# Two-input SBUF operations of a convolutional feed-forward: GpSimd's share given to VectorE, one convolution step to ScalarE

## The chip, the cores and the metric

The kernel runs on one core of a Trainium2 chip. The metric is the device time of one execution, in microseconds (us). A core has TensorE (PE, with its weight loads as PEld), VectorE (DVE), ScalarE (ACT), GpSimd (POOL) and SyncE (SP), each of which takes the instructions of its own queue in order.

## The reference, cut to what matters

Two attention layers and one mixing layer come first; the change lies in the last block, a feed-forward with a causal convolution of three taps over time:

```python
D_FF, FFN_CONV = 2816, 3
def conv_ffn(h, w_up, conv_w, conv_b, w_down):      # h: 1024 x 1024
    up, gv = jnp.split(h @ w_up, 2, axis=-1)        # w_up: 1024 x 5632
    up = causal_dwconv(up, conv_w, conv_b)          # y[t] = b + sum_i w[i] x[t-2+i], per channel
    return (jax.nn.gelu(up) * gv) @ w_down          # w_down: 2816 x 1024
# x = x + conv_ffn(rmsnorm(x, mlp_norm), ...); return rmsnorm(x, final_norm)
```

## The kernel before, in words

All arithmetic keeps float32 accuracy: an operand is split into a rounded part (`...h`, cast by ScalarE) and the rest (`...l` = operand minus rounded part, one two-input subtraction), and `mm3` (L125) issues three matmuls for a product (L127 to L129).

Both products of the feed-forward use seven block products in place of eight (a Strassen-Winograd scheme), so there are sums of blocks besides the splits. `up_sums` (L2076) makes the four sums of the activations once, T1 to T4, in four steps `k`; each step writes its sums into one tile `tz` of which there is a single buffer (tag `fxs`), and splits them into `ft1h/l` to `ft4h/l`. `ffn` (L2109) then goes through 11 rounds `j` of 256 channels. Round 0 is computed with plain products (`plain`, L2179). In each later round, for the half that is convolved (`i = 0`) and the gate half (`i = 1`): `load` fetches a 1 MB block `wraw` of the weights (two buffers), `sums` (L2137) makes the block sums in place and four splits `w1` (1024 columns), `ws2`, `ws1` (512 each), `w3` (1024) and `w4` (512) through `split_up` (L2032), and `prods` (L2158) issues 84 matmuls and takes the results out of PSUM into `fup` or `fg` with copies on ScalarE and sums on VectorE (L2167, L2173, L2175). The convolution (L2210 to L2212) and the gelu (L2213) follow for two tiles of 128 x 1024, then the sums of the down-weights `draw` (L2220 to L2223; the tile shares the one `fxs` buffer), the product with the gate (L2228), the sums of the result (L2231 to L2234) and the stores to DRAM tiles `fx` and `fy`.

The down product (L2259 on) loads one 128 x 512 piece of each operand per step `k` (`drx`, `dry`), splits both (`operands`, L2262), multiplies into eight PSUM banks (`fda`, `fdb`) and ends with the final norm (`final_norm`, L2041).

The order of the instructions on each engine is not that of the text: a scheduler orders them at build time by an estimate of when each can start. Tiles are reused through semaphores, per tile.

Before the change GpSimd has: the splits of `w1`, `ws1` and `w3` and those of `plain` and of the two weight blocks split ahead in the mixing layer (L2038); T3 and the splits of T3 and T4; the four `draw` sums; the split of the second operand of the down product (`dyl`, L2272); and two small memsets per round and a product of the final norm, which stay.

Of the kernel before, what the change touches and what calls it, by code (L numbers as in the profile page):

```python
# [12 lines left out]
F32 = mybir.dt.float32  # L13
F32R = mybir.dt.float32r
I32 = mybir.dt.int32
AF = mybir.ActivationFunctionType
ALU = mybir.AluOpType
# [35 lines left out]
class Kern:  # L53
# [1975 lines left out]
            yh, yl = H[k // 4, n]  # L2029
            self.mm3(o, w[0][:, k], w[1][:, k], yh[:, k % 4], yl[:, k % 4], k == 0, k == 7)  # L2030

    def split_up(self, W, raw, bufs, eng=None):  # L2032
        nc = self.nc
        n = raw.shape[1]
        wh = W.tile([128, 8, 128], F32R, name="fwh", tag="fwh", bufs=bufs)[:, 0:n]
        wl = W.tile([128, 8, 128], F32R, name="fwl", tag="fwl", bufs=bufs)[:, 0:n]
        nc.scalar.copy(wh, raw)  # L2037
        (eng or nc.gpsimd).tensor_tensor(wl, raw, wh.bitcast(F32), ALU.subtract)  # L2038
        return wh, wl

    def final_norm(self, W, t, x, g, out):  # L2041
# [33 lines left out]

    def up_sums(self, R, H):  # L2076

        nc, V, G = self.nc, self.nc.vector, self.nc.gpsimd
        new = lambda nm: R.tile([128, 4, 512], F32R, name=nm)
        T = {i: (new(f"ft{i}h"), new(f"ft{i}l")) for i in (2, 1, 3, 4)}  # L2080

        def split(i, k, t, eng):
            h, l = T[i]
            nc.scalar.copy(h[:, k], t)
            eng.tensor_tensor(l[:, k], t, h[:, k].bitcast(F32), ALU.subtract)

        def steps(P):
            for k in range(4):
                y11h, y11l, y21h, y21l, y22h, y22l, y12h, y12l = (
                    z[:, k].bitcast(F32) for b in ((0, 0), (1, 0), (1, 1), (0, 1)) for z in H[b])  # L2090
                z = P.tile([128, 4, 512], F32, name="tz", tag="fxs", bufs=1)
                t1, t2, t3, t4 = (z[:, i] for i in range(4))
                V.tensor_tensor(t1, y12h, y11h, ALU.subtract)
                V.tensor_tensor(t1, t1, y12l, ALU.add)
                V.tensor_tensor(t1, t1, y11l, ALU.subtract)
                V.tensor_tensor(t2, y22h, t1, ALU.subtract)
                V.tensor_tensor(t2, t2, y22l, ALU.add)
                split(2, k, t2, V)
                split(1, k, t1, V)
                G.tensor_tensor(t3, y22h, y12h, ALU.subtract)  # L2100
                G.tensor_tensor(t3, t3, y22l, ALU.add)
                G.tensor_tensor(t3, t3, y12l, ALU.subtract)
                split(3, k, t3, G)
                V.tensor_tensor(t4, y21h, t2, ALU.subtract)
                V.tensor_tensor(t4, t4, y21l, ALU.add)
                split(4, k, t4, G)
        return T, steps

    def ffn(self, h, side, x_src, out):  # L2109
        nc, a, sm = self.nc, self.a, self.sm  # L2110
        V, G = nc.vector, nc.gpsimd
# [5 lines left out]
        xd = [self.dr.tile([128, 7, 512], F32, name=f"fx{j}") for j in range(NJ)]  # L2117
        yd = [self.dr.tile([128, 4, 512], F32, name=f"fy{j}") for j in range(NJ)]
        with self.pool("fw", not side) as FW:
# [3 lines left out]
            cw = F1.tile([128, 22, 3], F32, name="fcw")  # L2123
            nc.sync.dma_start(cw, a["mlp_conv_w_2"])
            cb = F1.tile([128, 22], F32, name="fcb")
# [11 lines left out]
            def sums(j, i, raw):  # L2137

                b = lambda g, f: raw[:, 4 * g:4 * g + 4, f * 128:f * 128 + 128]
                x11, x12, x21, x22 = b(0, 0), b(1, 0), b(0, 1), b(1, 1)  # L2140
                s2, s1 = b(2, 0), b(2, 1)
                fa = raw[:, 0:8, 0:128]
                w1 = self.split_up(F0, fa, 2)
                V.tensor_tensor(s1, x21, x22, ALU.add)
                V.tensor_tensor(s2, s1, x11, ALU.subtract)
                w2 = self.split_up(FW, s2, 2, V), self.split_up(FW, s1, 2)
                V.tensor_tensor(x21, x11, x21, ALU.subtract)
                w3 = self.split_up(F0, raw[:, 0:8, 128:256], 2)
                V.tensor_tensor(s2, x12, s2, ALU.subtract)
                w4 = self.split_up(FW, s2, 2, V)  # L2150
                return w1, w2, w3, w4

            def mm4(o, w, k0, y, first):
# [40 lines left out]
            for j in range(NJ):  # L2194
                if j:
                    raws = [load(j, 0), load(j, 1)]
                ups = [F1.tile([128, S + 2], F32, name="fup", tag="fup", bufs=2) for _ in range(2)]
                for u in ups:
                    G.memset(u[:, 0:2], 0.0)
                gs = [F1.tile([128, S], F32, name="fg", tag="fg", bufs=2) for _ in range(2)]  # L2200
                if j == 0:
                    t_steps(F1)
                    plain([ups[0][:, 2:], ups[1][:, 2:], gs[0], gs[1]])
                else:
                    prods(j, 0, sums(j, 0, raws[0]), ups[0][:, 2:], ups[1][:, 2:])
                cvs = []
                for i, up in enumerate(ups):
                    f = 2 * j + i
                    cv = F1.tile([128, S], F32, name="fcv", tag="fcv", bufs=2)
                    V.tensor_scalar(cv, up[:, 2:], cw[:, f, 2:3], cb[:, f:f + 1], ALU.mult, ALU.add)  # L2210
                    V.scalar_tensor_tensor(cv, up[:, 1:S + 1], cw[:, f, 1:2], cv, ALU.mult, ALU.add)
                    V.scalar_tensor_tensor(cv, up[:, 0:S], cw[:, f, 0:1], cv, ALU.mult, ALU.add)  # L2212
                    nc.scalar.activation(cv, cv, AF.Gelu_apprx_tanh)  # L2213
                    cvs.append(cv)

                z = F1.tile([128, 4, 512], F32, name="draw", tag="fxs", bufs=1)
                nc.sync.dma_start(z.rearrange("p (f n) c -> p f (n c)", f=2),
                                  wdn[j * 256:j * 256 + 256, :].rearrange("(f p) n -> p f n", p=128))
                y11, y12, y21, y22 = (z[:, q] for q in range(4))
                G.tensor_tensor(y11, y12, y11, ALU.subtract)  # L2220
                G.tensor_tensor(y12, y22, y12, ALU.subtract)  # L2221
                G.tensor_tensor(y22, y22, y11, ALU.subtract)
                G.tensor_tensor(y21, y21, y22, ALU.subtract)  # L2223
                nc.scalar.dma_start(yd[j], z)
                if j:
                    prods(j, 1, sums(j, 1, raws[1]), gs[0], gs[1])
                for cv, g in zip(cvs, gs):
                    V.tensor_tensor(cv, cv, g, ALU.mult)  # L2228
                z = F1.tile([128, 4, 512], F32, name="fxs", tag="fxs", bufs=1)
                x11, x21, x12, x22 = (cv[:, n * 512:n * 512 + 512] for cv in cvs for n in range(2))  # L2230
                V.tensor_tensor(z[:, 0], x21, x22, ALU.add)  # L2231
                V.tensor_tensor(x21, x11, x21, ALU.subtract)
                V.tensor_tensor(z[:, 1], z[:, 0], x11, ALU.subtract)
                V.tensor_tensor(z[:, 2], x12, z[:, 1], ALU.subtract)  # L2234
                for q, t in enumerate((cvs[0], cvs[1])):
                    nc.scalar.dma_start(xd[j][:, 2 * q:2 * q + 2].rearrange("p n c -> p (n c)"), t)
                nc.scalar.dma_start(xd[j][:, 4:7], z[:, 0:3])
# [5 lines left out]
            prod = [(0, wy(0, 0), "A", True, 0, 0), (2, wy(1, 0), "B", True, 0, 0), (5, ty(3), "A", False, 0, 1),  # L2243
                    (4, ty(0), "B", True, 1, 1), (1, ty(1), "A", False, 1, 1), (6, wy(1, 1), "B", False, 0, 1),
                    (3, ty(2), "A", False, 1, 0)]

            pre = []
            for k in range(2):
                raw = FW.tile([128, 12, 256], F32, name="wraw", tag="wraw", bufs=2)
# [9 lines left out]
            with self.pool("dn", side) as DN, self.psum(A=(1, 4), B=(1, 4)):  # L2259
                xa, acc = [], {}  # L2260

                def operands(q, k):  # L2262
                    if q == 0 and k < 2:
                        return pre[k]
                    res = []
                    for nm, src, eng in (("x", xd[k][:, prod[q][0]], V), ("y", prod[q][1](k), G)):
                        raw = DN.tile([128, 512], F32, name="dr" + nm, tag="dr" + nm, bufs=6)
                        nc.sync.dma_start(raw, src)
                        hi = DN.tile([128, 512], F32R, name=f"d{nm}h", tag=f"d{nm}h", bufs=13)
                        lo = DN.tile([128, 512], F32R, name=f"d{nm}l", tag=f"d{nm}l", bufs=13)  # L2270
                        nc.scalar.copy(hi, raw)  # L2271
                        eng.tensor_tensor(lo, raw, hi.bitcast(F32), ALU.subtract)  # L2272
                        res.append((hi, lo))
                    return res

# [11 lines left out]
                for q in range(6):  # L2287
# [13 lines left out]
                    for t in range(4):  # L2301
                        read(q, t)
                ops = [operands(6, k) for k in range(NJ)]

                def last(t):
# [133 lines left out]
```

## Time and profile before

| | |
|---|---|
| time, 3 runs | 2934.91 us median (2933.06 to 2941.24) |
| the profiled execution | 2937.08 us, of which the span from first to last instruction is 2935.3 us |
| TensorE busy | 2734.4 us, 93% of the span |
| VectorE busy | 1924.4 us, 66% |
| ScalarE busy | 1298.2 us, 44% |
| GpSimd busy | 1130.4 us, 39% |
| mean granted TensorE clock | 0.964 of full speed |

Times in the rows are in us from the start of the span; "mean ns" is for one instruction. The feed-forward begins at about 2220 us: the activations' sums and round 0 up to about 2300, rounds 1 to 10 up to about 2705, the down product from there to the end.

### The profile page before, as it was taken

The page shows a single profiled execution, that of the slowest core. Times are in us where ns is not written, and L with a number is a line of the kernel's source. Part 1 is how long each engine was busy: PE and PEld are TensorE (multiplying, and loading weights), DVE is VectorE, ACT ScalarE, POOL GpSimd, SP SyncE. Part 2 cuts the span into 40 slices and gives each one's busy share as a digit, 9 for nine tenths or more (in the row PEclk, how much of TensorE's full clock was granted, in tenths as well). Part 3 has the DMA queues.
Part 4 walks back from the last instruction along what each step waited for, and adds up shares of the span by engine and source line. Part 5 has one row for each costly group of instructions (what it writes and reads, how often), then busy time and mean ns, then how long its engine had stood idle before and what let it go on. Part 6 is the DMA issues. An engine that isn't in the chain of part 4 may idle for free. (4 is left out here: it accounts for less than half of the span.)

```text
span 2935.3 us, 42585 instructions
## 1 busy us (share of the span) xinstructions
PE 2734.4 (93%) x14978; PEld 2191.2 (75%) x14978; DVE 1924.4 (66%) x4235; ACT 1298.2 (44%) x2534; POOL 1130.4 (39%) x851
## 2 busy tenths in 40 slices
PE   7999999899998999989999998999998899998998
PEld 6987666676778998766767775798676677776787
DVE  4784627785567676367866568643688688886733
ACT  5562227675623652156767323224333233323544
POOL 2232215672222324136742204341205555455743
PEclk9999999999999999999999999899999899999999
DMA  7456762326573363534056732245531334443973
GB/s 225 110 138 209 210 173 78 108 71 166 172 264 100 100 168 100 159 111 112 33 150 182 254 120 74 83 110 180 185 109 51 133 144 151 152 156 143 332 208 108
DMA packets 316602, 427.61 MB, mean 146 GB/s; under 512 B 36658, under 2 KB 224162, under 8 KB 314980
## 3 DMA queue, kind: packets, MB, share of 16 engines
q1 hardware_dynamic: 294464, 366.91, 41.9%
q10 hardware_dynamic: 21924, 57.98, 5.1%
q8 instruction: 118, 1.93, 0.3%
q14 instruction: 96, 0.79, 0.1%
HBM read 291.55 MB, written 132.64 MB: 145 GB/s over the span
## 5 line engine op out<-in xcount | busy, mean ns | idle before, releaser
L794 ACT ACTIVATE P<-P,nb 128x1024 f32<-128x1024 f32 (+1 forms) x320 | 316.6, 991 | 119.4 <-DVE nb L787 93.1
L127 PE MATMUL pj<-wh,hh 128*128 128x384 f32 (+3 forms) x768 | 264.4, 346 | 1.8 <-ACT cr L624 1.0
L128 PE MATMUL pj<-wl,hh 128*128 128x384 f32 (+3 forms) x768 | 263.7, 344 | 0.0
L129 PE MATMUL pj<-wh,hl 128*128 128x384 f32 (+3 forms) x768 | 260.8, 344 | 0.0
L806 PE MATMUL ptp<-ident,P 128*128 128x128 f32 x1568 | 218.4, 277 | 9.0 <-ACT PT L808 5.7
L806 PEld LDWEIGHTS ptp<-ident,P 128*128 128x128 f32 x1568 | 180.1, 142 | 50.8 <-issue 19.1
L2038 POOL TENSOR_TENSOR fwl<-wraw,fwh 128x1024 fp32r<-128x1024 f32 (+1 forms) x64 | 157.7, 2465 | 116.9 <-ACT fwh L2037 116.9
L954 POOL TENSOR_TENSOR P<-P,cf 128x1024 f32<-128x1024 f32 x64 | 121.0, 1893 | 211.4 <-DVE cf L952 147.3
L162 POOL TENSOR_TENSOR wl<-raw,wh 128x384 fp32r<-128x384 f32 (+3 forms) x64 | 77.7, 1218 | 300.2 <-ACT wh L161 257.3
L808 ACT COPY PT<-ptp 128x512 f32<-128x512 f32 (+1 forms) x255 | 138.1, 554 | 68.7 <-PE ptp L806 51.2
L787 DVE CUSTOM_DVE_ANT_0 P<-sd,zero 128x1024 f32<-128x1024 f32 x128 | 153.8, 1216 | 20.3 <-PE sd L945 20.0
L127 PE MATMUL po<-wh,yh 128*128 128x512 f32 x384 | 153.2, 406 | 8.2 <-ACT yh L1548 5.0
L129 PE MATMUL po<-wh,yl 128*128 128x512 f32 x384 | 152.2, 403 | 5.3 <-DVE yl L1549 5.3
L128 PE MATMUL po<-wl,yh 128*128 128x512 f32 x384 | 154.4, 402 | 1.3 <-DVE wl L140 1.2
L955 POOL TENSOR_TENSOR P<-P 128x1024 f32<-128x1024 f32 x64 | 153.5, 2402 | 3.6
L128 PEld LDWEIGHTS pj<-wl,hh 128*128 128x128 f32 x768 | 146.1, 190 | 10.7 <-issue 5.2
L127 PEld LDWEIGHTS pj<-wh,hh 128*128 128x128 f32 x768 | 146.1, 190 | 9.0 <-ACT cr L624 1.3
L129 PEld LDWEIGHTS pj<-wh,hl 128*128 128x128 f32 x768 | 145.1, 190 | 8.1 <-issue 3.5
L2037 ACT CAST fwh<-wraw 128x512 fp32r<-128x512 f32 (+1 forms) x104 | 83.2, 801 | 150.8 <-PE fu L128 90.2
L787 DVE CUSTOM_DVE_ANT_0 P<-sm,zero 128x1024 f32<-128x1024 f32 x96 | 116.9, 1218 | 44.5 <-PE sm L129 38.1
L2272 POOL TENSOR_TENSOR dyl<-dry,dyh 128x512 fp32r<-128x512 f32 x75 | 109.7, 1477 | 84.6 <-ACT dyh L2271 84.4
L2272 DVE TENSOR_TENSOR dxl<-drx,dxh 128x512 fp32r<-128x512 f32 x75 | 79.9, 1091 | 92.6 <-ACT dxh L2271 88.6
(724 smaller groups left out, 7777.2 us busy)
## 6 DMA issues: line engine op xcount, KB each, us to landing
adaw<-in_ada_w_dram SPq DMA_DIRECT2D x48, 512.0 KB
wraw<-in_w_up_dram SPq DMA_DIRECT2D x20, 1024.0 KB
raw<-in_w_in_dram SPq DMA_DIRECT2D x76, 256.0 KB
drx<-fx SPq DMA_DIRECT2D x75, 256.0 KB
mn<-naT SPq DMA_DIRECT2D x72, 256.0 KB
nab<-in_na_rpb_dram SPq DMA_DIRECT2D x24, 576.0 KB
naT<-sgn SPq DMA_DIRECT2D x64, 192.0 KB
md<-dfT SPq DMA_DIRECT2D x96, 128.0 KB
```

What stands on the lines that cost most here:

```text
L127: mm(o, lh, rh, start=first, stop=False, **kw)
L128: mm(o, lh, rl, start=False, stop=False, **kw)
L129: mm(o, ll, rh, start=False, stop=last, **kw)
L787: nc.vector.tensor_tensor_reduce(out=P[:, :n], in0=src, in1=self.zero.to_broadcast([128, n]), op0=ALU.add, op1=ALU.min, scale=1.0, scalar= ...
L794: nc.scalar.activation(P[:, :n], P[:, :n], AF.Exp, bias=nb, scale=-1.0 if bias is None else 1.0, accum_out=sums)
L806: nc.tensor.transpose(T[:, j * 128:(j + 1) * 128], P[:, (c + j) * 128:(c + j + 1) * 128], self.ident)
L808: e(PT[:, c:c + m, q, :], T[:, 0:m * 128].rearrange("p (k t) -> p k t", k=m))
L954: nc.gpsimd.tensor_tensor(Ps[1], Ps[1], cf[:, 1:2].to_broadcast([128, S]), ALU.mult)
L955: nc.gpsimd.tensor_tensor(Ps[0], Ps[0], Ps[1], ALU.add)
L2037: nc.scalar.copy(wh, raw)
L2038: (eng or nc.gpsimd).tensor_tensor(wl, raw, wh.bitcast(F32), ALU.subtract)
L2272: eng.tensor_tensor(lo, raw, hi.bitcast(F32), ALU.subtract)
```

## The change

All two-input operations on SBUF tiles that GpSimd did in the feed-forward go to VectorE: the remaining splits of `split_up`, T3 and the splits of T3 and T4, the `draw` sums, and `dyl`. The convolution's first step (scale by a per-channel weight and add the bias) goes from VectorE to an activation with function Identity on ScalarE. Counts, tiles, buffers and transfers stay.

```diff
-    def split_up(self, W, raw, bufs, eng=None):
+    def split_up(self, W, raw, bufs):
...
         nc.scalar.copy(wh, raw)
-        (eng or nc.gpsimd).tensor_tensor(wl, raw, wh.bitcast(F32), ALU.subtract)
+        nc.vector.tensor_tensor(wl, raw, wh.bitcast(F32), ALU.subtract)
...
-        def split(i, k, t, eng):
+        def split(i, k, t):
             h, l = T[i]
             nc.scalar.copy(h[:, k], t)
-            eng.tensor_tensor(l[:, k], t, h[:, k].bitcast(F32), ALU.subtract)
+            V.tensor_tensor(l[:, k], t, h[:, k].bitcast(F32), ALU.subtract)
...
-                G.tensor_tensor(t3, y22h, y12h, ALU.subtract)
-                G.tensor_tensor(t3, t3, y22l, ALU.add)
-                G.tensor_tensor(t3, t3, y12l, ALU.subtract)
-                split(3, k, t3, G)
+                V.tensor_tensor(t3, y22h, y12h, ALU.subtract)
+                V.tensor_tensor(t3, t3, y22l, ALU.add)
+                V.tensor_tensor(t3, t3, y12l, ALU.subtract)
+                split(3, k, t3)
...
-                split(4, k, t4, G)
+                split(4, k, t4)
...
-                w2 = self.split_up(FW, s2, 2, V), self.split_up(FW, s1, 2)
+                w2 = self.split_up(FW, s2, 2), self.split_up(FW, s1, 2)
...
-                    V.tensor_scalar(cv, up[:, 2:], cw[:, f, 2:3], cb[:, f:f + 1], ALU.mult, ALU.add)
+                    nc.scalar.activation(cv, up[:, 2:], AF.Identity, bias=cb[:, f:f + 1], scale=cw[:, f, 2:3])
...
-                G.tensor_tensor(y11, y12, y11, ALU.subtract)
-                G.tensor_tensor(y12, y22, y12, ALU.subtract)
-                G.tensor_tensor(y22, y22, y11, ALU.subtract)
-                G.tensor_tensor(y21, y21, y22, ALU.subtract)
+                V.tensor_tensor(y11, y12, y11, ALU.subtract)
+                V.tensor_tensor(y12, y22, y12, ALU.subtract)
+                V.tensor_tensor(y22, y22, y11, ALU.subtract)
+                V.tensor_tensor(y21, y21, y22, ALU.subtract)
...
-                    for nm, src, eng in (("x", xd[k][:, prod[q][0]], V), ("y", prod[q][1](k), G)):
+                    for nm, src in (("x", xd[k][:, prod[q][0]]), ("y", prod[q][1](k))):
...
-                        eng.tensor_tensor(lo, raw, hi.bitcast(F32), ALU.subtract)
+                        V.tensor_tensor(lo, raw, hi.bitcast(F32), ALU.subtract)
```

## Rows read from the trace of the kernel before

**Rows 1.** The page's first part: busy time, share of span, instructions.
```profile
PE 2734.4 (93%) x14978; PEld 2191.2 (75%) x14978; DVE 1924.4 (66%) x4235; ACT 1298.2 (44%) x2534; POOL 1130.4 (39%) x851
```

**Rows 2.** Windows of the feed-forward: from:to, length, busy (instructions), clock, DMA.
```profile
core 0: us, PE busy (x) PEld busy (x) DVE busy (x) ACT busy (x) POOL busy (x), PEclk, DMA share, GB/s
...
2220.00:2260.00 40.00, 39.22 (x168) 31.30 (x168) 39.72 (x32) 15.30 (x21) 26.20 (x15) 1.00 0.23 69
2260.00:2300.00 40.00, 19.48 (x59) 14.19 (x60) 32.08 (x28) 12.13 (x20) 24.85 (x15) 0.66 0.18 64
...
2300.00:2700.00 400.00, 374.74 (x1588) 301.49 (x1587) 318.41 (x287) 131.10 (x189) 214.44 (x120) 0.98 0.41 148
2700.00:2745.00 45.00, 36.81 (x131) 28.85 (x131) 17.07 (x17) 15.30 (x25) 16.32 (x12) 0.84 0.82 306
2745.00:2936.00 191.00, 182.95 (x805) 151.05 (x803) 95.35 (x142) 91.27 (x175) 104.37 (x72) 0.98 0.60 191
```

**Rows 3.** Timeline of PE: start, duration, line, [idle before <-releaser].
```profile
2272.93 0.80 PE L127 MATMUL fc<-ft1h,fwh 128*128 128x512 f32 x1 [13.71 <-ACT fwh L2037]
...
2286.69 0.80 PE L127 MATMUL fu<-ft2h,fwh 128*128 128x512 f32 x1 [3.65 <-DVE fup L2167]
...
2337.84 0.80 PE L127 MATMUL fu<-ft2h,fwh 128*128 128x512 f32 x1 [5.05 <-DVE fup L2167]
...
2490.49 0.50 PE L129 MATMUL fu<-y00h,fwl 128*128 128x512 f32 x1 [1.70 <-POOL fwl L2038]
...
2531.17 0.50 PE L129 MATMUL fu<-y00h,fwl 128*128 128x512 f32 x1 [1.75 <-POOL fwl L2038]
```

**Rows 4.** Timeline of DVE, from round 2 and a steady round.
```profile
2330.51 3.34 DVE L2212 SCALAR_TENSOR_TENSOR fcv<-fup,fcw,fcv 128x1024 f32<-128x1024 f32 x1
2333.78 3.41 DVE L2228 TENSOR_TENSOR fcv<-fcv,fg 128x1024 f32<-128x1024 f32 x1
...
2464.53 3.07 DVE L2228 TENSOR_TENSOR fcv<-fcv,fg 128x1024 f32<-128x1024 f32 x1 [0.34 <-ACT fg L2177]
...
2468.24 0.68 DVE L2038 TENSOR_TENSOR fwl<-wraw,fwh 128x512 fp32r<-128x512 f32 x1
...
2471.25 1.78 DVE L2234 TENSOR_TENSOR fxs<-fcv,fxs 128x512 f32<-128x512 f32 x1
...
2477.39 1.28 DVE L2212 SCALAR_TENSOR_TENSOR fcv<-fup,fcw,fcv 128x1024 f32<-128x1024 f32 x1
...
2498.35 1.22 DVE L2228 TENSOR_TENSOR fcv<-fcv,fg 128x1024 f32<-128x1024 f32 x1
```

**Rows 5.** Timeline of POOL in the same steady round.
```profile
2464.09 2.43 POOL L2038 TENSOR_TENSOR fwl<-wraw,fwh 128x1024 fp32r<-128x1024 f32 x1 [2.82 <-ACT fwh L2037]
2470.68 1.80 POOL L2038 TENSOR_TENSOR fwl<-wraw,fwh 128x512 fp32r<-128x512 f32 x1 [4.16 <-ACT fwh L2037]
...
2481.30 1.29 POOL L2220 TENSOR_TENSOR draw<-draw 128x512 f32<-128x512 f32 x1 [2.46 <-issue]
...
2487.09 3.34 POOL L2038 TENSOR_TENSOR fwl<-wraw,fwh 128x1024 fp32r<-128x1024 f32 x1
```

**Rows 6.** Waits between 2300 and 2700: who for whom, total us, times, longest.
```profile
POOL fwl L2038 <- ACT fwh L2037: 113.6, 29, 9.0
...
DVE fwl L2038 <- PE fc L129: 27.3, 8, 3.5
...
PE fu L129 <- POOL fwl L2038: 13.1, 7, 2.6
```

**Rows 7.** Groups of DVE between 2300 and 2700: busy us, mean ns of one.
```profile
L2210 DVE TENSOR_SCALAR fcv<-fup,fcw,fcb 128x1024 f32<-128x1024 f32 x20 | 27.0, 1352 | 7.4 <-ACT fup L2177 7.2
```

**Rows 8.** Groups of ACT over the whole span.
```profile
L2213 ACT ACTIVATE fcv<-fcv 128x1024 f32<-128x1024 f32 x22 | 23.3, 1061 | 123.4 <-DVE fcv L2212 123.3
...
L207 ACT ACTIVATE xs<-xs,xrs 128x1024 f32<-128x1024 f32 x4 | 4.4, 1139 | 0.0
```

**Rows 9.** Groups from 2700 to the end: the down product's split on POOL.
```profile
L2272 POOL TENSOR_TENSOR dyl<-dry,dyh 128x512 fp32r<-128x512 f32 x75 | 109.7, 1477 | 84.6 <-ACT dyh L2271 84.4
```

More of the change, by code (lines that the diff above doesn't have):

```diff
@@ L2076, in up_sums @@
     def up_sums(self, R, H):
-        nc, V, G = self.nc, self.nc.vector, self.nc.gpsimd
+        nc, V = self.nc, self.nc.vector
         new = lambda nm: R.tile([128, 4, 512], F32R, name=nm)
         T = {i: (new(f"ft{i}h"), new(f"ft{i}l")) for i in (2, 1, 3, 4)}
-        def split(i, k, t, eng):
+        def split(i, k, t):
             h, l = T[i]
             nc.scalar.copy(h[:, k], t)
-            eng.tensor_tensor(l[:, k], t, h[:, k].bitcast(F32), ALU.subtract)
+            V.tensor_tensor(l[:, k], t, h[:, k].bitcast(F32), ALU.subtract)
         def steps(P):
@@ L2097, in steps @@
                 V.tensor_tensor(t2, t2, y22l, ALU.add)
-                split(2, k, t2, V)
-                split(1, k, t1, V)
-                G.tensor_tensor(t3, y22h, y12h, ALU.subtract)
-                G.tensor_tensor(t3, t3, y22l, ALU.add)
-                G.tensor_tensor(t3, t3, y12l, ALU.subtract)
-                split(3, k, t3, G)
+                split(2, k, t2)
+                split(1, k, t1)
+                V.tensor_tensor(t3, y22h, y12h, ALU.subtract)
+                V.tensor_tensor(t3, t3, y22l, ALU.add)
+                V.tensor_tensor(t3, t3, y12l, ALU.subtract)
+                split(3, k, t3)
                 V.tensor_tensor(t4, y21h, t2, ALU.subtract)
                 V.tensor_tensor(t4, t4, y21l, ALU.add)
-                split(4, k, t4, G)
+                split(4, k, t4)
         return T, steps
@@ L2149, in sums @@
                 V.tensor_tensor(s2, x12, s2, ALU.subtract)
-                w4 = self.split_up(FW, s2, 2, V)
+                w4 = self.split_up(FW, s2, 2)
                 return w1, w2, w3, w4
```

## The prediction, as it was written before the result

> **What bounds the kernel now.** I read the page's first part, then windows of the stretch that the change touches, then the timelines of TensorE, VectorE and GpSimd there, and last the table of waits. The page says that TensorE is busy 93% of the span [rows 1], so only TensorE's idle time and its slow time can be won, and the other engines count only through them. The windows say where that is [rows 2]: from 2220 to 2300, 21.3 of 80 us are idle (80 minus 39.22 and 19.48); from 2300 to 2700, 25.3 of 400 are; from 2700 to 2745, 8.2 of 45; after it 8.1 of 191, which lie in the final norm's tail, where nothing changes. The reader should see in the same rows the granted clock: 0.66 from 2260 to 2300 and full speed before. That window begins to starve TensorE (one wait of 13.71 us [rows 3]) and the clock is low behind it, so idle time costs twice. At full clock 168 matmuls took 39.22 us, 0.233 each; 59 took 19.48 in the slow window instead of 13.8, a loss of 5.7. For 2300 to 2700 I price the slow time by the clock, 0.98: 2% of 374.74 is 7, of which I count 5, since the rounding allows 3.7 to 9. What can be won is thus 21.3 + 5.7 = 27 in the first stage and 25.3 + 5 = 30 in the rounds, 57 in all.
>
> Who holds TensorE up? Steady rounds begin 40.7 us apart (2490.49 to 2531.17), and the one stall in each is 1.7 us for the rest part of a weight split that GpSimd makes [rows 3]; seven of these make 13.1 us [rows 6]. In the early rounds it waits for VectorE: 5.05 us at 2337.84 for a sum (L2167) [rows 3] that stood on VectorE behind an L2212 of 3.34 and an L2228 of 3.41 us [rows 4]. In the first stage it waits for the sums T and for a cast that stands on ScalarE behind casts of T [rows 3].
>
> The last thing to see is that VectorE is slow when GpSimd works. The same L2228 takes 3.07 us at 2464.53, where GpSimd subtracts from 2464.09 to 2466.52, and 1.22 at 2498.35 where GpSimd is idle; a 512-column sum takes 1.78 at 2471.25, with GpSimd at work from 2470.68 to 2472.48, and 0.68 at 2468.24 without [rows 4, 5]. GpSimd suffers too: its 1024-column split takes 2.43 or 3.34 us [rows 5].
>
> **The change part by part.** *The rounds.* From the code, VectorE has in a round 22 operations of 512 columns, two L2228, four convolution steps L2211 and L2212, and two L2210. Alone these cost 22 x 0.68 + 2 x 1.22 + 4 x 1.28 = 22.5 us [rows 4], and L2210 2 x 1.35 as it stands now [rows 7]: 25.2. It is in fact busy 318.41 / 400 x 40.7 = 32.4 us a round [rows 2], so some 7 us of a round are stretch. The change adds six operations of 512 columns (two `ws1`, four `draw`) and four of 1024 (`w1`, `w3`): 6 x 0.68 + 4 x 1.22 = 9.0 us. It takes L2210 away. With GpSimd left with only memsets, VectorE needs 22.5 + 9.0 = 31.5 of 40.7 us: about what it is busy now, for more work. So no new bound by the sum.
>
> What it gives TensorE: a 1024-column split comes 1.22 us after its cast in place of 2.43 to 3.34, and is not behind a `draw` sum on GpSimd; the gain in latency, 1.2 to 2.1, is as large as the stall of 1.7. I take 11 of the 13.1 us. The other 12.2 of idle time in the rounds (25.3 - 13.1) are waits like that at 2337.84; there the two stretched operations ahead of the sum shrink by 2.06 + 2.19 = 4.2 us, against a wait of 5.05. I take 9 of 12.2, and 3 of the 5 us of slow clock with them: 23.
>
> What is new: VectorE takes its queue in order. A `draw` sum now stands in it until its transfer has landed; GpSimd stood 2.46 us for that at 2481.30 [rows 5]. What is queued behind are splits and the sum L2167 that TensorE wants next. Per round the cost is nothing if the scheduler puts the sum late enough, and at most 2.5 us, 25 for ten rounds. I take 0.6 a round, nearer to nothing, because VectorE has 9.2 us to spare in a round: 6. The rounds give 23 - 6 = 17.
>
> *The first stage, 2220 to 2300.* VectorE is busy 71.8 of 80 us [rows 2]. From the code, the four steps of `up_sums` have 14 two-input operations each, of which five move; with round 0 and the first sums of round 1 that is about 71 operations of 512 columns, 7 of 1024 and 4 convolution steps after the change, 71 x 0.68 + 7 x 1.22 + 4 x 1.28 = 62 us. VectorE sets the pace of T here before and after, because the single `tz` buffer chains the four steps. I add 6 us for casts of ScalarE inside a step (now some 8 us are idle). 80 - 68 = 12 us sooner; the bounds are nothing (each step gated by something else) and the 27 us above. I take 12, low clock included.
>
> *The convolution on ScalarE.* An activation with two per-channel operands on 128 x 1024 took 1.14 us at L207, a gelu 1.06 [rows 8]. Two a round bring ScalarE from 131.1 / 400 x 40.7 = 13.3 to 15.6 us a round [rows 2], so its sum hides it. On the chain to the gelu it replaces 1.35 by 1.14 plus a hop between engines. What could be late is a copy from PSUM queued behind it: at most 1.14 us for each tile, 20 tiles, 23 us if nothing covered it; I take nothing because L2213 alone waits 123.4 us for the convolution [rows 8], idle time in which the first step fits.
>
> *The down product, the mixing layer, the gap between.* `dyl` takes 1.48 us on GpSimd [rows 9] and 0.68 on VectorE; per step VectorE has two, 1.4 us, against 12 matmuls of 0.233 = 2.8. The windows from 2745 on have no idle time beyond the tail [rows 2], and before 2745 the transfers are 0.82 busy: nothing won, up to 3 if the last round's tail shortens. The two splits in the mixing layer add 2.4 us on VectorE: nothing, at most 2.4 lost.
>
> Sum: 17 + 12 = 29 us off the profiled 2937.1, 2908. The median of the runs stands 2.2 lower, so 2906.
>
> **A rule against it.** The Trainium skill, Perfetto Trace Analysis, section Optimizing Scalar/DVE Operations, says that where VectorE is saturated it may pay to hand work to ScalarE or even GpSimd, though it warns that GpSimd and VectorE share a read port. Read by the first half, VectorE at 80% in the rounds [rows 2] is nearly saturated and taking work back would lengthen them, which is the second rival below; the rows with GpSimd idle bear out the second half.
>
> **The rivals.**
> 1. *Waits in order on VectorE (slower).* GpSimd now waits 113.6 us in these 400 for casts of ScalarE [rows 6], 11.6 a round, and 2.5 for the `draw` load. These would become VectorE's, beside the 2.8 a round in which it already waits for a buffer that TensorE holds (27.3 [rows 6]). Its spare time is 9.2 - 2.8 = 6.4 a round; beyond 6.4 us of inherited waits the round gets longer. With two thirds of the 14.1 it would be 9.4, a round of 43.7 and ten of them 30 us longer; the first stage's 12 us remain: 2953. For it: the scheduler's estimates are not the chip's (GpSimd does stand at the head of its queue). Against: GpSimd waits because it has nothing else, and an order made for VectorE would put other work first. Chance 0.09.
> 2. *The stretch stays (slower).* If VectorE is slow there for another reason than GpSimd (the transfers, TensorE's reads), its sum is 32.4 - 2.7 + 9.0 = 38.7 a round, with 2.8 of waits 41.5: 0.8 us over the round, it becomes the bound from 40.7 on, and the stalls stay: 8 us slower, 2943. If the moved operations stretched too, far more. Against: the pairs of rows 4 and 5. Chance 0.04.
> 3. *The stalls move (no change).* TensorE's waits for GpSimd become waits for VectorE of the same length and the first stage gains only some: 4 to 8 us, half of them given back, 2926 to 2940, centre 2931. Chance 0.13.
> 4. *Nearly all is won.* First stage 27, rounds 28: 2937.1 - 55 - 2.2 = 2880. For it: VectorE's 31.5 of 40.7. Against: one tile `tz`, and the early rounds wait for loads as well. Chance 0.09.
>
> **How the numbers follow.** My forecast has 0.65; its own range is 2890 to 2924, from 12 + 33 and from 5 + 6 us won (draw at its full price in the second). The four rivals share 0.35. A range for 8 in 10 leaves out the two slower rivals (0.13), and some of rivals 3 and 4: 2881 to 2934. Under 0.3%, 8.8 us, a measurement of this kernel tells nothing (its three runs span 8.2 us). Faster, below 2926: 0.65 + 0.09 and a little of rival 3, 0.75. Slower, above 2943.7: rival 1 and about half of rival 2, with a little of 3: 0.12. The same: 0.13.
>
> **What would show it.** Right: GpSimd nearly without work after 2220; L2228 at 1.2 us and 512-column sums at 0.7 everywhere; VectorE still some 32 us a round; no wait of TensorE for a split; steady rounds 39.2 us apart (168 x 0.233); the window from 2260 with a higher clock and round 1 beginning some 12 us sooner. The prediction is wrong if VectorE shows idle time ahead of `draw` sums or splits with TensorE waiting behind (rival 1), if L2228 still takes 2 to 3 us with GpSimd idle (rival 2), or if the convolution's first step on ScalarE holds up copies from PSUM.

## The result, and the profile after

The median of four runs is 2902.44 us (2897.13 to 2909.21), beside 2933.98 for the kernel before in the same comparison: a ratio of 0.990 with an interval of 0.988 to 0.992, so faster by 31.5 us. The profiled execution took 2901.85 us, its span 2900.1. The forecast was 2906.

The page's first part shows what moved. VectorE has 183 instructions more than before and is busy 30 us less; GpSimd loses a third of its time [rows 1].

```profile
PE 2733.7 (94%) x14978; PEld 2188.9 (75%) x14978; DVE 1894.7 (65%) x4418; ACT 1323.1 (46%) x2556; POOL 749.3 (26%) x646
```

Windows of the feed-forward after, in the columns of [rows 2]:

```profile
2220.00:2260.00 40.00, 39.76 (x176) 32.00 (x175) 37.04 (x60) 20.29 (x27) 0.20 (x2) 1.00 0.29 93
2260.00:2300.00 40.00, 34.70 (x136) 26.37 (x135) 33.60 (x51) 14.27 (x24) 0.00 (x0) 0.91 0.23 83
2300.00:2700.00 400.00, 388.94 (x1658) 314.54 (x1656) 289.06 (x373) 160.46 (x219) 1.78 (x18) 0.98 0.48 171
2700.00:2745.00 45.00, 40.49 (x167) 33.15 (x166) 35.27 (x56) 32.32 (x54) 0.00 (x0) 0.92 0.96 341
```

From 2260 to 2300 TensorE starts 136 matmuls where it started 59, at a granted clock of 0.91 where it was 0.66. In the rounds it is idle 11 of 400 us where it was 25, and VectorE, with eight operations more in a round, is busy 289 us where it was 318.

Timeline of TensorE after, idle time in brackets (the two L1977 rows are the mixing layer, the others the feed-forward):

```profile
2139.16 0.30 PE L1977 MATMUL gyT<-ident,goo 128*128 128x128 f32 x1 [2.98 <-DVE goo L1975]
...
2205.13 0.30 PE L1977 MATMUL gyT<-ident,goo 128*128 128x128 f32 x1 [1.67 <-DVE goo L1975]
...
2280.94 0.80 PE L127 MATMUL fc<-ft1h,fwh 128*128 128x512 f32 x1 [4.65 <-ACT ft1h L2084]
...
2321.04 0.50 PE L129 MATMUL fu<-y00h,fwl 128*128 128x512 f32 x1 [1.86 <-DVE fwl L2038]
...
2340.01 0.79 PE L129 MATMUL fc<-ft1h,fwl 128*128 128x512 f32 x1 [2.95 <-DVE fwl L2038]
...
2666.67 0.50 PE L127 MATMUL fu<-ft4h,fwh 128*128 128x512 f32 x1 [1.10 <-DVE fg L2173]
```

The wait of 13.71 us at the first `fc<-ft1h` [rows 3] is gone; the 4.65 at 2280.94 is a later one, for a cast of T1, which was 3.39 before. Between 2340.01 and 2666.67 no wait of TensorE shows: the 1.7 us in every steady round are gone. Steady rounds are 38.66 us apart (40.7 before).

To see where the time went I cut the span at five points, taken from four rows that every kernel has: the last L1454 on VectorE, the first matmul `fu<-y01h`, the first and last `fu<-ft4h`, the first `fda<-dyh`. Their rows after (instructions, duration, first to last start):

```profile
L1454 DVE TENSOR_TENSOR xo<-po,xo x8: 1210/1220/1225, 2051.4 to 2109.8; 128x1024 f32<-128x1024 f32 x8
...
L127 PE MATMUL fu<-y01h,fwh x4: 389/389/497, 2227.0 to 2229.6; 128*128 128x512 f32 x4
...
L127 PE MATMUL fu<-ft4h,fwh x80: 389/389/501, 2297.4 to 2668.8; 128*128 128x512 f32 x80
...
L127 PE MATMUL fda<-dyh,dxh x168: 389/389/796, 2679.2 to 2891.9; 128*128 128x512 f32 x168
```

| us, one profile each | up to L1454 | end of the mixing layer | first stage | rounds | down and tail | `fu<-y01h` to the end |
|---|---|---|---|---|---|---|
| before | 2107.5 | 112.4 | 90.2 | 393.1 | 221.4 | 715.4 |
| after | 2109.8 | 117.2 | 70.4 | 371.4 | 220.9 | 673.1 |

The feed-forward is 42.3 us shorter, 19.8 of it in the first stage and 21.7 in the rounds. The end of the mixing layer takes 4.8 us more, and the part that nothing touches 2.3 more: 42.3 - 4.8 - 2.3 = 35.2, the difference of the spans.

The border between first stage and rounds needs a correction, because the scheduler put TensorE's matmuls in another order. From the first `fu<-y01h` up to the first `fu<-ft4h` there are 252 matmuls in the kernel before and in e1, e7 and e8 (the experiments below), 264 after and in e2 to e5, and 276 in e6; twelve matmuls are 2.8 us of work. Cut after 276 matmuls instead, first stage and rounds in the columns of [rows 2], two rows before and two after:

```profile
2219.89:2315.63 95.74, 71.98 (x276) 55.91 (x277) 79.34 (x65) 30.80 (x45) 60.98 (x35) 0.84 0.22 73
2315.63:2703.16 387.53, 364.73 (x1547) 293.56 (x1546) 310.99 (x280) 127.84 (x184) 205.22 (x114) 0.98 0.41 149
...
2226.96:2300.19 73.23, 67.93 (x276) 53.10 (x277) 66.59 (x97) 32.79 (x48) 0.20 (x2) 0.95 0.26 87
2300.19:2668.84 368.65, 361.38 (x1546) 292.72 (x1545) 275.72 (x354) 151.25 (x204) 1.78 (x18) 0.99 0.45 159
```

For the same number of matmuls the first stage is 22.5 us shorter and the rounds are 18.9 shorter.

Groups of VectorE and ScalarE from 2300 to 2660 after (columns as in [rows 7]):

```profile
L2038 DVE TENSOR_TENSOR fwl<-wraw,fwh 128x1024 fp32r<-128x1024 f32 x36 | 44.0, 1222 | 34.7 <-ACT fwh L2037 34.3
L2038 DVE TENSOR_TENSOR fwl<-wraw,fwh 128x512 fp32r<-128x512 f32 x53 | 36.3, 685 | 7.0 <-ACT fwh L2037 6.5 <-PE fc L129 0.5
...
L2228 DVE TENSOR_TENSOR fcv<-fcv,fg 128x1024 f32<-128x1024 f32 x18 | 21.8, 1218 | 0.0
...
L2210 ACT ACTIVATE fcv<-fup,fcb,fcw 128x1024 f32<-128x1024 f32 x20 | 24.9, 1248 | 30.6 <-DVE fxs L2234 25.7 <-DVE fup L2175 4.7
```

Every VectorE operation is at its short time: L2228 has a mean of 1218 ns, and took 3.07 or 3.41 us where GpSimd worked [rows 4].

Waits from 2200 to the end after: who for whom, total us, times, longest. These are VectorE's own, in order ahead of what TensorE wants next; six of the seven for `draw` lie between 2424 and 2618, where TensorE waits for nothing.

```profile
DVE fwl L2038 <- ACT fwh L2037: 43.6, 27, 3.2
...
DVE wraw L2144 <- DMA wraw<-in_w_up_dram: 23.4, 11, 9.1
...
DVE draw L2220 <- DMA draw<-in_w_down_dram: 12.1, 7, 3.7
```

### The profile page after: what moved, and what is told of

It reads as the page before. It is cut to its first block, busy times and chain, and to the rows that moved or that the text cites. A ratio compares the mean times of both kernels' runs of the same rounds, so it can differ in the third digit from the quotient of the medians.

```text
span 2900.1 us, 42531 instructions
## 1 busy us (share of the span) xinstructions
PE 2733.7 (94%) x14978; PEld 2188.9 (75%) x14978; DVE 1894.7 (65%) x4418; ACT 1323.1 (46%) x2556; POOL 749.3 (26%) x646
## 5 line engine op out<-in xcount | busy, mean ns | idle before, releaser
L787 DVE CUSTOM_DVE_ANT_0 P<-sm,zero 128x1024 f32<-128x1024 f32 x96 | 116.9, 1217 | 45.1 <-PE sm L129 38.8
L808 DVE COPY PT<-ptp 128x512 f32<-128x512 f32 (+1 forms) x161 | 105.2, 657 | 50.8 <-PE ptp L806 36.8
L2038 DVE TENSOR_TENSOR fwl<-wraw,fwh 128x512 fp32r<-128x512 f32 (+1 forms) x104 | 94.7, 912 | 44.6 <-ACT fwh L2037 43.6
```

The lines of the kernel that those rows point to most:

```text
L787: nc.vector.tensor_tensor_reduce(out=P[:, :n], in0=src, in1=self.zero.to_broadcast([128, n]), op0=ALU.add, op1=ALU.min, scale=1.0, scalar= ...
L808: e(PT[:, c:c + m, q, :], T[:, 0:m * 128].rearrange("p (k t) -> p k t", k=m))
L2038: nc.vector.tensor_tensor(wl, raw, wh.bitcast(F32), ALU.subtract)
```

## The experiments

Eight kernels were run. The theory: GpSimd's reads from SBUF stretch VectorE's two-input operations, so taking them away shortens everything on VectorE that TensorE waits for. Its rivals: the gain is the shorter latency of the splits alone; it is the convolution step's move; or only VectorE's order counts. The stages of all profiles, cut as in the table above (not corrected for the order of the matmuls):

| kernel | median, us | ratio to before (95%) | mixing end | first stage | rounds | to the end |
|---|---|---|---|---|---|---|
| e1, step to ScalarE alone | 2919.1 | 0.9966 (0.9952 to 0.9981) | 112.5 | 86.5 | 380.3 | 696.4 |
| e2, moves without that step | 2892.7 | 0.9877 (0.9844 to 0.991) | 117.4 | 70.6 | 367.5 | 669.5 |
| e3, after with idle subtractions on GpSimd | 2956.2 | 1.0091 (1.0065 to 1.0118) | 116.9 | 82.9 | 420.5 | 733.8 |
| e4, after with idle memsets on GpSimd | 2900.9 | 0.989 (0.9868 to 0.9911) | 118.7 | 70.5 | 369.1 | 670.3 |
| e5, e2 with the two early splits on GpSimd | 2884.6 | 0.9847 (0.982 to 0.9873) | 111.1 | 71.9 | 362.7 | 665.6 |
| e6, before with T3 and splits of T3, T4 moved | 2915.9 | 0.9953 (0.994 to 0.9966) | 112.6 | 78.2 | 384.7 | 692.9 |
| e7, before with the rounds' splits moved | 2898.6 | 0.990 (0.9873 to 0.9928) | 112.5 | 76.2 | 372.0 | 678.5 |
| e8, before with the `draw` sums moved | 2934.1 | 1.0006 (0.9988 to 1.0024) | 112.4 | 86.5 | 391.9 | 708.9 |

**e1 and e2: the convolution's step and the moves, each alone.** e1 is the kernel before with L2210 on ScalarE; e2 is the changed kernel with L2210 back.

```diff
-                    V.tensor_scalar(cv, up[:, 2:], cw[:, f, 2:3], cb[:, f:f + 1], ALU.mult, ALU.add)
+                    nc.scalar.activation(cv, up[:, 2:], AF.Identity, bias=cb[:, f:f + 1], scale=cw[:, f, 2:3])
```

> The kernel before, with only the convolution's first step moved to ScalarE; all of GpSimd's work stays. Theory (GpSimd's work and its stretch of VectorE is what cost the time): the steady rounds stay near 40.7 us with a stall of some 1.7 us for GpSimd's split in each, the first stage is still starved, VectorE's two-input operations are still stretched; 0 to 8 us faster than before. Rival (what helped is that VectorE lost the convolution's first step): 20 us or more faster than before.

> The changed kernel with the convolution's first step back on VectorE. Theory: VectorE carries 1.6 us more a round (0.8 each, alone) of about 39 us and has room for it; within 6 us of the changed kernel (2896 to 2909). Rival (ScalarE's step is needed for the gain): 2920 or more.

e1 was 14 us faster than before, more than the 0 to 8 expected. The stall of 1.7 us in a steady round shrinks to 0.69. That the rest comes sooner because a disturbed VectorE has two operations less a round is a likely reason, but not shown: the orders of GpSimd's and TensorE's queues changed in the rounds too. One of its rows; from 2300 to 2660 seven such waits sum to 7.5 us (13.1 [rows 6]).

```profile
2494.66 0.50 PE L129 MATMUL fu<-y00h,fwl 128*128 128x512 f32 x1 [0.69 <-POOL fwl L2038]
```

e2 came out at 2892.7, somewhat under the 2896 to 2909 expected, so the moves alone give the whole gain and the step on ScalarE adds nothing to them. Its group on VectorE from 2300 to 2660 tells why:

```profile
L2210 DVE TENSOR_SCALAR fcv<-fup,fcw,fcb 128x1024 f32<-128x1024 f32 x20 | 16.1, 809 | 0.3
```

With GpSimd out of the way the step takes 0.81 us on VectorE, beside 1.35 in the kernel before [rows 7] and 1.25 on ScalarE after. Whether the step on ScalarE costs something stays open: steady rounds are 38.67 us in e2 too, so the 3.9 us between 371.4 and 367.5 arise in the other rounds; e2 and e5 differ there by 4.8 with the same program in the rounds; and the intervals of e2 and of the changed kernel overlap.

**e3 and e4: give GpSimd work again that nobody waits for.** Both are the changed kernel with a private tile in SBUF. In each round from 1 on GpSimd subtracts it from itself 14 times (e3), or clears it 30 times (e4), behind one sum of two columns that ties it to the round (round 0 has that sum alone).

```diff
+            scr = F1.tile([128, 512], F32, name="scr")
+            G.memset(scr, 0.0)
...
+                G.tensor_tensor(scr[:, 0:2], scr[:, 0:2], ups[0][:, 0:2], ALU.add)
+                if j:
+                    for _ in range(14):
+                        G.tensor_tensor(scr, scr, scr, ALU.subtract)
```

```diff
+                    for _ in range(30):
+                        G.memset(scr, 0.0)
```

> The changed kernel with added work on GpSimd that nobody waits for: in each of rounds 1 to 10, 14 two-input subtractions of a private 128 x 512 tile from itself, about 20 us a round, as much as GpSimd did before. TensorE's order is unchanged. Theory (the two engines hold each other up): VectorE's operations with two SBUF inputs stretch again, 512 columns from 0.68 to over 1 us on average, the gate product from 1.22 to 2 or more, VectorE's busy time from 289 in 400 us to over 340, while sums with a PSUM operand stay at 0.68; TensorE's stalls return in part, 5 to 30 us slower than the changed kernel. Rival (the gain was only that splits are made sooner and that GpSimd's queue is out of the way): VectorE stretches or not, the time stays within 4 us of the changed kernel.

> The same with memsets in place of the subtractions: 30 of the private 128 x 512 tile a round, which only write. Theory that what VectorE and GpSimd compete for is reading SBUF: no operation of VectorE is stretched, and the time is within 4 us of the changed kernel. Rival (any work of GpSimd slows VectorE): stretched like with the subtractions, and a like loss of time.

The subtractions cost 53.8 us against the changed kernel, more than the 5 to 30 expected, and leave it slower than before, although VectorE's operations stretch less on the mean than expected (0.90 us for over 1, 1.53 for 2 or more). TensorE is idle 37.2 us in the 360 from 2300, and 6.2 in the changed kernel. The memsets cost nothing. Groups from 2300 to 2660 of e3 (its lines stand 2 to 6 further down; L2234 is L2228, L2228 a `draw` sum, L2175 the sum L2173 that reads PSUM):

```profile
L2038 DVE TENSOR_TENSOR fwl<-wraw,fwh 128x512 fp32r<-128x512 f32 x48 | 43.4, 904 | 5.1 <-ACT fwh L2037 4.2 <-PE fc L129 0.9
...
L2234 DVE TENSOR_TENSOR fcv<-fcv,fg 128x1024 f32<-128x1024 f32 x16 | 24.4, 1532 | 0.0
...
L2228 DVE TENSOR_TENSOR draw<-draw 128x512 f32<-128x512 f32 x9 | 11.9, 1327 | 0.1
...
L2175 DVE TENSOR_TENSOR fg<-fu,fg 128x512 f32<-128x512 f32 x8 | 5.4, 678 | 0.0
...
L2205 POOL TENSOR_TENSOR scr<-scr 128x512 f32<-128x512 f32 x112 | 159.4, 1424 | 8.2
```

And of e4:

```profile
L2038 DVE TENSOR_TENSOR fwl<-wraw,fwh 128x512 fp32r<-128x512 f32 x55 | 37.8, 687 | 6.7 <-ACT fwh L2037 5.7 <-PE fc L129 1.0
...
L2234 DVE TENSOR_TENSOR fcv<-fcv,fg 128x1024 f32<-128x1024 f32 x18 | 21.9, 1220 | 0.0
...
L2205 POOL MEMSET scr<- 128x512 f32 x270 | 142.4, 527 | 15.1
```

GpSimd is about equally busy in both, 159 and 142 us of 360, and TensorE, VectorE and ScalarE execute the same instructions in the same order as in the changed kernel, so neither order nor the splits' engine differs. Where it reads SBUF, VectorE's operations with two inputs there are stretched (904 for 687 ns, 1532 for 1220); where it only writes, none is, and the sums that take one input from PSUM keep their 0.68 us in both. This pair settles the cause of the stretch: no engine shows a wait for these subtractions, and writes alone do no harm, so what is left is the engines' competition for reading SBUF. The Trainium skill says this of the two engines (SBUF — State Buffer, section Who interferes with whom): a VectorE instruction with two SBUF inputs contends with a GpSimd instruction that reads SBUF, not with one that only writes; both runs agree. A piece of the timelines of e3 shows how TensorE comes to wait:

```profile
2451.22 0.68 DVE L2038 TENSOR_TENSOR fwl<-wraw,fwh 128x512 fp32r<-128x512 f32 x1
...
2453.28 11.12 POOL L2205 TENSOR_TENSOR scr<-scr 128x512 f32<-128x512 f32 x8
...
2453.62 1.52 DVE L2038 TENSOR_TENSOR fwl<-wraw,fwh 128x512 fp32r<-128x512 f32 x1
...
2460.85 0.68 DVE L2175 TENSOR_TENSOR fg<-fu,fg 128x512 f32<-128x512 f32 x1
...
2461.59 0.50 PE L127 MATMUL fu<-ft4h,fwh 128*128 128x512 f32 x1 [3.73 <-DVE fg L2175]
```

The same split takes 0.68 us before GpSimd's eight subtractions and 1.52 within them. The sum L2175, itself 0.68, is late because of the stretched operations ahead of it (and 0.73 us in which VectorE waits for a load), and TensorE stands 3.73 us. This is the pattern of [rows 4] at 2330, brought back by work without a consumer.

The rows also say what the stretch is: not slow work, but a wait for the end of GpSimd's instruction. L2228 at 2464.53 ends 1.08 us after the split on GpSimd in which it began, and the sum at 2471.25 ends 0.55 us after its own [rows 4, 5]. Over all such pairs in before, e1, e3 and e6 to e8, the median is 1.08 us for two-input operations of 1024 columns and 0.55 for those of 512. So the length of GpSimd's single instruction counts: 1.42 us in e3, up to 3.34 before [rows 5], which fits the smaller mean stretch in e3.

Not settled by it: how much of the 31.5 us comes from these waits, and how much from splits that no longer take 2.43 or 3.34 us on GpSimd. No run separates the two.

**e6, e7 and e8: the parts of the move, each alone on the kernel before.**

```diff
-                G.tensor_tensor(t3, y22h, y12h, ALU.subtract)
...
-                split(4, k, t4, G)
+                V.tensor_tensor(t3, y22h, y12h, ALU.subtract)
...
+                split(4, k, t4, V)
```

```diff
-                w1 = self.split_up(F0, fa, 2)
+                w1 = self.split_up(F0, fa, 2, V)
...
-                w2 = self.split_up(FW, s2, 2, V), self.split_up(FW, s1, 2)
+                w2 = self.split_up(FW, s2, 2, V), self.split_up(FW, s1, 2, V)
...
-                w3 = self.split_up(F0, raw[:, 0:8, 128:256], 2)
+                w3 = self.split_up(F0, raw[:, 0:8, 128:256], 2, V)
```

```diff
-                G.tensor_tensor(y11, y12, y11, ALU.subtract)
...
+                V.tensor_tensor(y11, y12, y11, ALU.subtract)
...
```

> The kernel before, with only T3 and the splits of T3 and T4 on VectorE. Theory: the first stage alone gets shorter: from the first matmul of round 0 to the first matmul with ft4 (90 us before, 70 after the whole change) 70 to 82; the rounds keep their 40.7 us and their stalls; 8 to 18 us faster than before. Rival (the first stage is gated by the splits of the weights on GpSimd): 86 us or more, and no faster.

> The kernel before, with only the splits of w1, ws1 and w3 in the rounds on VectorE; T, the draw sums and the split of the down product stay on GpSimd. Theory: the stall of 1.7 us a round for GpSimd's split goes, and GpSimd is left with some 7 us of draw sums a round, so VectorE is stretched little: steady rounds 39 to 40 us, 8 to 20 us faster than before. Rival (VectorE, still disturbed by the draw sums, becomes the bound): rounds of 41 us or more, slower than before.

> The kernel before, with only the four draw sums of each round on VectorE. Theory: GpSimd's split of 1024 columns no longer stands behind a draw sum, so the stall of 1.7 us a round goes or halves; VectorE gets 2.7 us more work a round and is still stretched by the splits; between 5 us slower and 15 us faster than before. Rival (VectorE waits at the head of its queue for the load of the draw tile): stalls of TensorE for VectorE of over 1.7 us a round, slower than before by 5 us or more.

e7 alone, the splits of `w1`, `ws1` and `w3`, gives as much as the whole change (0.990 both; 32 us, where 8 to 20 were expected): 21.1 us in the rounds and 14.0 in the first stage, although the `draw` sums stay on GpSimd, which is busy 72 of the 360 us from 2300. e6 is 15 us faster: by the table 12.0 in the first stage and 8.4 in the rounds, but 17.5 and 2.9 when both kernels are cut after 276 matmuls. e8 gives no time at all, although GpSimd was freed for its splits. One of TensorE's waits in e8 and two groups of VectorE, 2300 to 2660, then a piece of its timelines:

```profile
PE fu L127 <- DVE fg L2167: 12.0, 8, 1.7
...
L2221 DVE TENSOR_TENSOR draw<-draw 128x512 f32<-128x512 f32 x10 | 21.2, 2122 | 0.0
L2220 DVE TENSOR_TENSOR draw<-draw 128x512 f32<-128x512 f32 x10 | 20.7, 2073 | 18.4 <-DMA draw<-in_w_down_dram 18.4
...
2481.36 2.42 POOL L2038 TENSOR_TENSOR fwl<-wraw,fwh 128x1024 fp32r<-128x1024 f32 x1 [1.95 <-ACT fwh L2037]
...
2481.76 2.56 DVE L2220 TENSOR_TENSOR draw<-draw 128x512 f32<-128x512 f32 x1 [2.52 <-DMA draw<-in_w_down_dram]
...
2484.25 0.68 DVE L2167 TENSOR_TENSOR fg<-fu,fg 128x512 f32<-128x512 f32 x1
```

TensorE's 13.1 us for GpSimd's split [rows 6] became 12.0 for a sum of VectorE, L2167. In VectorE's queue it now stands behind the first `draw` sum, which waits for its load (18.4 us in all) and then, held up by GpSimd's split, takes 2.56 us, about four times its own 0.68. This is rival 3 in pure form; in the changed kernel, where GpSimd reads nothing there, the waits for the `draw` load are up to 3.7 us long and cost TensorE nothing. The parts don't add up: in the first stage, cut after 276 matmuls, e1, e6, e7 and e8 win 3.7, 17.5, 14.0 and 3.7 us, 38.9 together, and the whole 22.5. e6 and e7 end the same wait, that of 13.71 us [rows 3]: the longest left there is 1.8 us in e6 and 4.7 in e7, while e1 and e8 keep one of 12.7 and 13.5.

**e5: the best of these.** The two splits in the mixing layer go back to GpSimd, for which TensorE shows no wait there in the kernel before, and L2210 to VectorE.

```diff
-                    self.ff0.append(self.split_up(N["F"], raw[t // 2 - 1], 2))
+                    self.ff0.append(self.split_up(N["F"], raw[t // 2 - 1], 2, nc.gpsimd))
...
-    def split_up(self, W, raw, bufs):
+    def split_up(self, W, raw, bufs, eng=None):
...
-        nc.vector.tensor_tensor(wl, raw, wh.bitcast(F32), ALU.subtract)
+        (eng or nc.vector).tensor_tensor(wl, raw, wh.bitcast(F32), ALU.subtract)
...
-                    nc.scalar.activation(cv, up[:, 2:], AF.Identity, bias=cb[:, f:f + 1], scale=cw[:, f, 2:3])
+                    V.tensor_scalar(cv, up[:, 2:], cw[:, f, 2:3], cb[:, f:f + 1], ALU.mult, ALU.add)
```

> The changed kernel with two parts undone: the two weight splits made ahead in the mixing layer are on GpSimd again, and the convolution's first step on VectorE. Theory: the stretch of the mixing layer from its last sum L1454 to the first matmul of round 0, 112.4 us before the change and 117 to 119 in the four profiles with these splits on VectorE, returns to 112 to 113, and the rest is as in the kernel with the moves only; 4 to 6 us faster than that one, 2885 to 2892. Rival (the 5 us come from something else, such as where the profile falls): 117 or more, no faster than with the moves only.

2884.6 us, 46 faster than before in its comparison, where the change won 31.5 in its own; the intervals of the two ratios don't overlap. The end of the mixing layer is back at 111.1 us. In its window of the rounds TensorE is idle 3.5 of 360 us, at full clock:

```profile
2300.00:2660.00 360.00, 356.51 (x1546) 290.11 (x1545) 289.54 (x373) 126.97 (x183) 1.79 (x18) 1.00 0.45 160
```

## Why the prediction was right, point by point

The time was forecast 3.6 us high (2906 for 2902.4), for the reason given: GpSimd's reads stretch VectorE, and VectorE paces TensorE. The terms were less exact than their sum, and that the sum came so near is in part luck: the feed-forward won 42.3 us where 29 were forecast, and the 4.8 us lost in the mixing layer and 2.3 us of drift in a part that nothing touches took some of it back.

**The rounds.** Forecast -17, measured -21.7 by the table and -18.9 for the same number of matmuls. Of the 18.9, TensorE's idle time makes 15.5 (22.8 to 7.3 us), and a granted clock of 0.99 in place of 0.98 the remaining 3.4. The forecast had 23 for these two (20 idle, 3 clock), 4 too many, before it took 6 away for `draw` sums that wait for their load. These waits exist, 12.1 us in seven places, twice the 6 assumed, but none is followed by a wait of TensorE: VectorE has the time. This price was the mis-sized part of the term, and the two errors cancel in part. (For the slow clock, 0.98 as a rounded number allows 5.6 to 9.4 us, not 3.7 to 9.) VectorE is busy 269.18 / 360 x 38.67 = 28.9 us a round (31.5 forecast). The forecast added whole durations, but an operation starts some 0.07 us before the one ahead of it has ended: in [rows 4], 2330.51 + 3.34 is 2333.85, and the next starts at 2333.78. For 38 operations that is 2.7 us. The steady round of 39.2 was 38.66.

**The first stage.** Forecast -12, measured -19.8 by the table and -22.5 for the same number of matmuls, within the bounds of 0 and 27 but nearly twice the forecast: the term that was furthest off. The twelve us were counted for VectorE's sum over the four steps of T. Without the same 0.07 us for its 82 operations that sum would have given 18, and e6, which moves T3 and the splits of T3 and T4, gives 17.5. What the sum left out is that the splits of the first rounds count there as well: e7 wins 14.0 us with T untouched, whether by the splits' own time or by VectorE's fewer waits for GpSimd.

**The convolution's step.** Forecast nothing; nothing shown in company of the moves. One step of its working was wrong: "it replaces 1.35 by 1.14" took a stretched duration for VectorE's. Undisturbed it is 0.81, so the step became slower by 0.44 us on the chain to the gelu, which TensorE did not feel in the steady rounds.

**The down product.** Forecast nothing, measured -0.5.

**The mixing layer.** Forecast "nothing, at most 2.4 lost"; measured 4.8 lost. Here the term was mis-sized, because it priced two operations by their durations and not by what queues behind them, nor by a new order of the queue. Timelines of VectorE and ScalarE after (the last two rows belong to the rivals, below):

```profile
2134.18 1.23 DVE L2038 TENSOR_TENSOR fwl<-fraw,fwh 128x1024 fp32r<-128x1024 f32 x1 [1.85 <-ACT fwh L2037]
2135.33 0.15 DVE L123 SCALAR_TENSOR_TENSOR grs<-nwt,grs 128x4 f32<-128x4 f32 x1
...
2138.67 1.13 DVE L1975 SCALAR_TENSOR_TENSOR goo<-goo,grs,gg 128x128 f32<-128x128 f32 x4
...
2203.50 1.23 DVE L1487 TENSOR_TENSOR xo<-po,xo 128x1024 f32<-128x1024 f32 x1 [0.91 <-PE po L129]
2204.64 1.13 DVE L1975 SCALAR_TENSOR_TENSOR goo<-goo,grs,gg 128x128 f32<-128x128 f32 x4
...
2331.86 0.69 DVE L2144 TENSOR_TENSOR wraw<-wraw 128x512 f32<-128x512 f32 x1 [9.07 <-DMA wraw<-in_w_up_dram]
...
2335.66 0.62 ACT L2037 CAST fwh<-wraw 128x512 fp32r<-128x512 f32 x1 [4.22 <-DVE fcv L2232]
```

The split stands 1.85 us at the head of VectorE's queue for its cast and then takes 1.23; behind it is `grs`, which L1975 needs, and TensorE waits 2.98 us for L1975 at 2139.16 (row of the timeline above). The other wait, 1.67 us at 2205.13, has no split near it: there L1975 stands behind an L1487 that itself waits 0.91 us for TensorE. The scheduler gave VectorE and TensorE another order in this part. The kernel before has no wait for `goo` L1975 there. How much of the 4.8 us is the split's wait and how much the new order is not shown. In the profiles of e2 to e4 and after, with these splits on VectorE, this part takes 116.9 to 118.7 us, in the other six 111.1 to 112.6, and e5 takes the splits back, which also brings back TensorE's order of before in this part, and with them the loss is gone.

**The rivals.** Rival 1 (waits in order on VectorE) did not come true for the waits that the change brings to the rounds. Its mechanism showed in two places: in the mixing layer, with a part of the 4.8 us, and once in the first rounds, where VectorE stands 9.07 us for a load of `wraw`; it waited for such loads before the change too, up to 6.4 us. Behind it stands L2232, for which ScalarE's cast waits 4.22 us, and TensorE's last waits until 2340.01 follow, some 3.5 us (0.50 for the cast at 2336.33 and 2.95 for the split). Rival 2 (the stretch has another cause) is refuted by the 1218 ns of L2228 and by e3 against e4. Rival 3 (the stalls move) is what e8 does, and what the whole change does not. Rival 4 was too much for this kernel, by 22 us, and e5 comes within 5 us of it. Of the rule that was weighed against the change, that work of a busy VectorE may go to ScalarE or GpSimd, e3 shows the GpSimd half to be dear here; of the ScalarE half, e1 shows 14 us of gain while GpSimd still reads, and e2 none once VectorE is undisturbed.

## What to carry to other kernels

When GpSimd reads SBUF beside VectorE's two-input operations, price its work by what it does to VectorE, not by its own time: compare the same VectorE instruction with GpSimd at work and idle, as in [rows 4, 5], and see whether its end keeps a fixed distance from the end of GpSimd's instruction. Don't expect the parts of such a move to add up, or each to gain: here the splits that TensorE waited for gave as much alone as all together (e7), and the `draw` sums alone gave nothing (e8). Take a duration for a sum from the undisturbed state that the change makes, for the operations that stay as for those that move, and from start to start where operations follow each other. Before stages of two kernels are compared, count the instructions in them: the scheduler may have moved some across the border. Before a split is put on an engine that has an order of its own to keep, look at what stands behind it in that queue while its input is late: GpSimd's wait there cost nothing.

## What was not expected of the hardware

- Work without a consumer cost a quarter of its duration: 140 subtractions on GpSimd, 199.5 us in the whole span, made the kernel 53.8 us slower.
- Memsets of the same tile, 142.4 us of them in 360, cost nothing that can be measured.
- The operation held up need not have two tiles as inputs: L2210 reads one, takes 0.80 us alone and had a mean of 1.35 before [rows 7]; at 2401.89 it took 2.78 us, begun within a split on GpSimd from 2401.23 to 2404.12.
- The part of the kernel up to L1454, in which all kernels do the same, took from 2101.5 us (e3) to 2118.1 us (e1) in ten single profiles. Single spans can so differ by up to 16.6 us for a reason that is not in the change, which is why stages are compared here and medians given for times. What moves this part was not found.
